# Attention's queries and keys split into high and low parts behind their projections, stored so, with memory of its own for every second pair of heads

## The chip, the core and the metric

The kernel runs on one core of a Trainium2 chip. Four of its engines compute: PE (matrix products, with PEld, the loading of the stationary operand, beside it), DVE (vector work), ACT (activation functions and scaled copies) and POOL. SP mostly issues transfers. Each engine works through its own instructions in the order in which they stand, and waits where an operand, or the memory that it writes, isn't free; what stands behind a waiting instruction waits too. The metric is the device time of one execution in microseconds (us), the median of several runs.

## What is computed

One decoder layer on 1024 tokens of width 1024, in float32. After a normalisation one projection gives the columns of two groups of heads: eight attention heads (queries, keys and values, 64 wide each) and eight heads of a recurrent mixer (RWKV-7). Both results are joined, projected (`w_out`), added to the input, and a feed-forward block follows.

```python
h = _rms_norm(x, norm_mix_pre[i])
z = h @ w_in_first
q = z[..., 0:D_ATTN]; k = z[..., D_ATTN:2 * D_ATTN]; v = z[..., 2 * D_ATTN:3 * D_ATTN]
...
attn = _rms_norm(_dilated_attention(q, k, v), attn_out_gain[i])   # causal, masked scores / sqrt(64)
rw = _rwkv7(r_r, k_r, v_r, ...)
x = x + _rms_norm(jnp.concatenate([attn, rw], axis=-1) @ w_out[i], norm_mix_post[i])
f = jnp.square(jax.nn.relu(_rms_norm(x, norm_ffn_pre[i]) @ w_ffn_up[i])) @ w_ffn_down[i]
x = x + _rms_norm(f, norm_ffn_post[i])
```

## The kernel before, in words

**Split operands.** A float32 product is made from parts in the faster type fp32r: a high part (a copy that rounds) and a low part (the difference). For the big products three matmuls add up high x high, low x high and high x low (`mm3`). Attention's scores need two: for each head the tile `qs` holds in its partitions 0 to 63 the high part of the scaled query and in 64 to 127 its low part, and `kh` and `kl` hold the key's high and low part in both halves, so that one matmul against `kh` and one against `kl` give all four products.

**Stages.** The program runs through the projections with the recurrent mixer woven in, attention, the output projection with the two normalisations (`pm`, `mxa`, `mxr`, `h2t`), and the feed-forward block up (`X`, `Y`, `Z`) and down (`dX`, `dY`, `dZ`).

**Projections.** Each slab of 128 columns is projected in two halves of 512 tokens, 24 matmuls each, into a PSUM bank of the tag `z` (two banks). `proj_spill` empties the bank: for attention's slabs (`aq`, `ak`, `av`, four of each, numbers 12 to 23) ACT copies the half into an SBUF tile of the tag `ev` (three buffers, shared with the mixer's values), and an ACT-queue transfer stores it in DRAM (`zs_d`). A planner (`drive`) that counts estimated times writes down in which order PE takes the mixer's pieces and the projections. PE's order is as written, there and in attention; the order on the other engines, SP among them, is made by a scheduler from the dependencies and priorities.

**Attention.** The eight heads are four pairs p = 0 to 3. A pair has 16 steps m: eight blocks i of 128 queries times two heads h. For a step `at_s` makes the scores (two matmuls into `pS` for each 512 keys; DVE adds the mask `stripT` and keeps the minimum in one instruction; ACT takes the exponential of the row S and its sum), `at_t` turns the row by PE transposes into `pT`, in banks `a` and `c`, one each, which ACT (bank `a`) and DVE (bank `c`, from the fourth block on) copy to `PT`. After every second block `at_v` multiplies by the values into `po`. Scores are made two steps ahead of the transposes, within a pair; at a pair's end, the next pair's first two scores stand behind the last transposes. The values of a pair are loaded as `vT` and turned (`vt`, `Vt`) by `at_vt`.

**Loading a pair** (`at_load`). For each head two transfers bring the query from `zs_d` into both halves of a tile `qr`. POOL writes the scaled high part to `qs` (line 855), DVE overwrites its lower half by the difference (line 856). Two transfers bring the key into `kr`, POOL writes `kh` (line 132), DVE writes `kl` (line 865). The tiles `raw`, `qs`, `kh`, `kl` have two buffers for each tag, one for each head, so that a tile of the next pair can be written only when the last scores of the present pair have read it. `at_load(p + 1)` stands at step 1 of pair p.

**Woven in.** Between attention's steps PE takes the rest of the last projection (steps 0 to 7), and in pairs 2 and 3 parts of the output projection that need only the mixer (`r_ahead`, matmuls `pm`). The weights of the output projection (`WO`) are loaded and split at fixed steps by `load_wo`; four of them, and the tiles of the mix, lie where the projection's input `hT` was (`open_mix`).

Of the kernel before, what the change touches and what calls it, by code (L numbers as in the profile page):

```python
# [8 lines left out]
F32 = mybir.dt.float32  # L9
# [31 lines left out]
def hybrid_kernel(tc, x, par, cst, strip, win, wup_lora, gup, gnwb, grow, wout, wup, wdown, out, dbg=None):  # L41
# [22 lines left out]
    with (  # L64
# [52 lines left out]
        bk_d = dp.tile([8, P, 2, 4, P], F32, name="bk_d")  # L117
        v_d = dp.tile([S, 512], F32, name="v_d")
# [228 lines left out]
        def gate():  # L347
            for t in range(8):
                pg = ps.tile([P, 512], F32, name=f"g{t}", tag="w")
                tt = slice(t * P, (t + 1) * P)  # L350
                mm3(pg, sgh[:, tt], sgl[:, tt], gh, gl, True, True)
                go = evp.tile([P, 512], F32, name=f"go{t}", tag="ev", bufs=3)
                A.activation(go, pg, AF.Copy)
                nc.scalar.dma_start(g_d[t * P:(t + 1) * P, :], go)
                yield 0.7, 0.7
# [318 lines left out]
        def v_out(p, hf):  # L674
# [8 lines left out]
            vt = evp.tile([P, 512], F32, name=f"vt{p}_{hf}", tag="ev", bufs=3)  # L683
            vc = evp.tile([P, 512], F32, name=f"vc{p}_{hf}", tag="ev", bufs=3)
# [8 lines left out]
        def proj_spill(nm, i, shift):  # L693
            last = [None]

            def ev(hf, pz):
                zt_ = evp.tile([P, 512], F32, name=f"ev_{nm}_{hf}", tag="ev" if i >= 8 else "kr", bufs=3 if i >= 8 else 8)
# [147 lines left out]
        at, sx, pts, pos = {}, {}, {}, {}  # L845

        def at_load(p):

            QS, KH, KL = [], [], []
            for h in range(2):  # L850
                qr = ap_.tile([P, S], F32, name=f"qr{p}_{h}", tag="raw")
                for d in range(2):
                    nc.sync.dma_start(qr[own[d]], zs_d[12 + p, h * 64:h * 64 + 64, :])
                qs = ap_.tile([P, S], F32R, name=f"qs{p}_{h}", tag="qs")
                G.tensor_scalar(qs, qr, -0.125, 0.0, op0=OP.mult, op1=OP.add)
                V.scalar_tensor_tensor(qs[64:128], qr[64:128], -0.125, qs[64:128].bitcast(F32), OP.mult, OP.subtract)
                QS.append(qs)
            for h in range(2):
                kr = ap_.tile([P, S], F32, name=f"kr{p}_{h}", tag="raw")
                for d in range(2):  # L860
                    nc.sync.dma_start(kr[own[d]], zs_d[16 + p, h * 64:h * 64 + 64, :])
                kh = ap_.tile([P, S], F32R, name=f"kh{p}_{h}", tag="kh")
                kl = ap_.tile([P, S], F32R, name=f"kl{p}_{h}", tag="kl")
                gcopy(kh, kr)
                V.tensor_tensor(kl, kr, kh.bitcast(F32), OP.subtract)
                KH.append(kh)
                KL.append(kl)
            at[p] = QS, KH, KL

        def at_vt(p):  # L870
            vT = ap_.tile([P, S], F32, name=f"vT{p}", tag="raw")
# [8 lines left out]
        def at_s(p, i, h):  # L880
# [9 lines left out]
            for k in range(nbk):  # L890
                lo, hi = 512 * k, min(w, 512 * k + 512)
                pS = ps.tile([P, 512], F32, name=f"pS{p}_{i}_{h}_{k}", tag="wz"[k] if p == 1 or p == 2 and i < 6 else "w")
# [62 lines left out]
        def open_mix():  # L955
            ev_ctx.__exit__(None, None, None)
            left.__exit__(None, None, None)
            M["tc"] = tc.tile_pool(name="tcomb", bufs=1)
            M["tp"] = M["tc"].__enter__()
            M["mc"] = tc.tile_pool(name="mix", bufs=2)  # L960
            M["mp"] = M["mc"].__enter__()
# [31 lines left out]
        def mix_x1(t, pm, y=None):  # L993
# [5 lines left out]
            if y is None:  # L999
                y = mp.tile([P, D], F32, name=f"y{t}", tag="y")  # L1000
# [58 lines left out]
        def r_ahead(i, keep):  # L1059
# [14 lines left out]
            part[i] = M["mp"].tile([P, D], F32, name=f"y{ORD[i]}", tag="y")  # L1074
# [4 lines left out]
        LEAD = 28  # L1079
        for _ in range(LEAD):  # L1080
            next(rest, None)
        hi_pri = lambda: tc.high_priority(offset=PRI[3])
        step = lambda m: (m // 16, m % 16 // 2, m % 2)
        with hi_pri():
            at_load(0)
            at_s(*step(0))
            at_s(*step(1))
            at_vt(0)
        for m in range(64):
            p, i, h = step(m)  # L1090
            with hi_pri():
                if i == 7:
                    at_t(p, i, h)
                    if h == 0:
                        at_v(p, 4)
                    else:
                        if p < 3:
                            at_s(p + 1, 0, 0)
                            at_s(p + 1, 0, 1)
                            at_v(p, 6)  # L1100
                            at_vt(p + 1)
                else:
                    at_s(p, (m % 16 + 2) // 2, h)
                    at_t(p, i, h)
                    if h == 1 and i in (2, 4):
                        at_v(p, i - 2)
                    if h == 1 and i == 0 and p < 3:
                        at_load(p + 1)
# [5 lines left out]
            if m in (13, 21) or m in (29, 37):  # L1114
                k = {13: 4, 21: 5, 29: 6, 37: 7}[m]
                load_wo(k, w2p, "w2")
            if m == 31:
                open_mix()
            if m in (43, 45, 47, 49):
                load_wo((m - 43) // 2, M["tp"], "woA")  # L1120
            for i_, m0 in ((0, 45), (1, 53)):
# [11 lines left out]
        tp, tp_ctx, mp, mix_ctx = M["tp"], M["tc"], M["mp"], M["mc"]  # L1133
# [120 lines left out]
        mix_ctx.__exit__(None, None, None)  # L1254
        if "x1" in dbg:
# [261 lines left out]
```

## Time and profile before

| | |
|---|---|
| median of three runs | 1368.56 us (1368.4 to 1368.89) |
| the profiled execution | 1369.49 us, its span from the first to the last instruction 1367.7 us |
| busy in the span | PE 1291.0 us (94%), DVE 914.4 us, ACT 626.3 us, POOL 45.9 us |
| PE busy, 200 to 500 us (projections) | 287.4 of 300 us |
| PE busy, 500 to 600 us (attention) | 78.4 of 100 us |
| PE busy, 800 to 1300 us (feed-forward) | 499.6 of 500 us |
| granted PE clock, 500 to 600 us | 0.93; 1.00 from 650 to 1300 us |

The profile gives one execution. A row of the timeline shows when a group of equal instructions started, how long it ran from its first start to its last end, and in brackets how long the engine stood idle before it and what ended that wait. Matmuls overlap, so a row's duration reaches a little into the next row. The chain of waits follows the program back from its last instruction to what released each step; in it a stretch of matmuls has just the time that it adds.

### The profile page before, as it was taken

The page shows a single profiled execution, that of the slowest core. Times are in us where ns is not written, and L with a number is a line of the kernel's source. Part 1 is how long each engine was busy: PE and PEld are TensorE (multiplying, and loading weights), DVE is VectorE, ACT ScalarE, POOL GpSimd, SP SyncE. Part 2 cuts the span into 40 slices and gives each one's busy share as a digit, 9 for nine tenths or more (in the row PEclk, how much of TensorE's full clock was granted, in tenths as well). Part 3 has the DMA queues.
Part 4 walks back from the last instruction along what each step waited for, and adds up shares of the span by engine and source line. Part 5 has one row for each costly group of instructions (what it writes and reads, how often), then busy time and mean ns, then how long its engine had stood idle before and what let it go on. Part 6 is the DMA issues. An engine that isn't in the chain of part 4 may idle for free.

```text
span 1367.7 us, 23518 instructions
## 1 busy us (share of the span) xinstructions
PE 1291.0 (94%) x9360; PEld 1063.5 (78%) x9360; DVE 914.4 (67%) x1647; ACT 626.3 (46%) x1026; POOL 45.9 (3%) x56
## 2 busy tenths in 40 slices
PE   6999999999999988789998999999999999999997
PEld 5777888788777867678787788888888888888875
DVE  7867757531678576555698986777666776445686
ACT  7652324233455376455556444444343444443442
POOL 0000000000000101010000000000000002000110
PEclk9999999999999999999999999999999999999999
DMA  6346747676584663321333344443456995346554
GB/s 253 114 169 162 193 107 195 184 203 211 169 248 147 200 211 91 86 70 40 123 123 133 137 169 170 153 145 135 161 200 211 327 349 182 92 128 210 187 204 165
DMA packets 161197, 231.09 MB, mean 169 GB/s; under 512 B 51680, under 2 KB 88800, under 8 KB 161088
## 3 DMA queue, kind: packets, MB, share of 16 engines
q1 hardware_dynamic: 153024, 208.62, 47.2%
q10 hardware_dynamic: 8064, 20.98, 4.5%
q8 instruction: 73, 1.20, 0.4%
q14 instruction: 36, 0.29, 0.1%
HBM read 156.66 MB, written 72.89 MB: 168 GB/s over the span
## 4 chain that ended last, share of the span: by engine, by line
PE 74%; DVE 13%; DMA 6%; ACT 4%; issue 2%; SPq 0%; POOL 0%; DVEq 0%; ACTq 0%; POOLq 0%
PE X L47 11%; PE dX L47 8%; PE Z L47 6%; PE pm L47 6%; PE dZ L47 5%; PE z_aq L47 3%; PE dY L47 3%; PE z_av L47 3%; PE po L47 3%; PE z_ak L47 3%; PE Y L47 3%; PE z_v L47 3%; PE z_k L47 3%; PE pT L908 2%; PE pS L47 2%
## 5 line engine op out<-in xcount | busy, mean ns | idle before, releaser
L47 PE MATMUL dX<-wow,wou 128*128 128x512 f32 x768 | 176.2, 390 | 2.3 <-DVE wow L1179 1.6
L47 PEld LDWEIGHTS dX<-wow,wou 128*128 128x128 f32 x768 | 143.8, 188 | 34.1 <-DVE wow L1179 3.4
L47 PE MATMUL dZ<-wow,wou 128*128 128x512 f32 x384 | 87.4, 389 | 0.0
L47 PEld LDWEIGHTS dZ<-wow,wou 128*128 128x128 f32 x384 | 72.1, 188 | 15.0
L1178 ACT ACTIVATE wow<-wd 128x1024 fp32r<-128x1024 f32 x40 | 42.3, 1060 | 88.9 <-PE dZ L47 29.8
L1179 DVE TENSOR_TENSOR wou<-ur,wou 128x1024 fp32r<-128x1024 f32 x56 | 72.0, 1287 | 8.4 <-ACT wou L1178 8.3
L1179 DVE TENSOR_TENSOR wow<-wd,wow 128x1024 fp32r<-128x1024 f32 x40 | 49.9, 1250 | 34.7 <-ACT wow L1178 34.1
L1178 ACT ACTIVATE wou<-ur 128x1024 fp32r<-128x1024 f32 x56 | 58.5, 1048 | 20.9 <-DMA ur<-u_d 13.4
L908 PE MATMUL pT<-cst,S 128*128 128x128 f32 x288 | 47.1, 290 | 18.4 <-DVE PT L912 12.2
L898 ACT ACTIVATE S<-S,mn 128x128 f32<-128x128 f32 (+7 forms) x64 | 49.4, 772 | 19.2 <-DVE mn L896 18.4
L908 PEld LDWEIGHTS pT<-cst,S 128*128 128x128 f32 x288 | 34.4, 146 | 28.7 <-issue 11.1
L1265 ACT ACTIVATE r<-u 128x512 f32<-128x512 f32 x48 | 30.0, 626 | 52.4 <-DVE u L1263 52.0
L896 DVE CUSTOM_DVE_ANT_0 S<-pS,stripT 128x512 f32<-128x512 f32 (+3 forms) x64 | 37.6, 590 | 23.5 <-PE pS L47 18.6
L47 PE MATMUL pm<-WO,mxr 128*128 128x512 f32 x192 | 49.4, 400 | 0.5 <-DVE mxr L972 0.5
L47 PE MATMUL z_aq<-hT,wh_aq 128*128 128x512 f32 x128 | 46.5, 417 | 3.5 <-DVE ev_v L202 3.5
L1179 DVE TENSOR_TENSOR wow<-TK,wow 128x1024 fp32r<-128x1024 f32 x16 | 20.8, 1301 | 38.9 <-ACT wow L1178 38.9
L47 PE MATMUL z_k<-hT,wh_k 128*128 128x512 f32 x128 | 44.9, 412 | 1.7 <-DVE z L233 1.4
L47 PE MATMUL Z<-HB,wo 128*128 128x512 f32 x192 | 46.1, 389 | 0.0
L47 PE MATMUL pm<-WO,mxa 128*128 128x512 f32 x192 | 45.8, 394 | 0.0
L47 PE MATMUL X<-HB,wo 128*128 128x512 f32 x180 | 43.6, 390 | 1.6 <-ACT HB L1034 1.6
L47 PE MATMUL z_av<-hT,wh_av 128*128 128x512 f32 x128 | 44.9, 405 | 0.0
L910 ACT ACTIVATE PT<-pT 128x512 f32<-128x512 f32 (+3 forms) x64 | 32.8, 512 | 26.0 <-PE pT L908 17.2
(388 smaller groups left out, 3097.0 us busy)
## 6 DMA issues: line engine op xcount, KB each, us to landing
ur<-u_d SPq DMA_DIRECT2D x56, 512.0 KB, 4.3
wd<-in_wdown_dram SPq DMA_DIRECT2D x40, 512.0 KB, 4.2
u_d<-S SPq DMA_DIRECT2D x64, 256.0 KB, 2.1
u_d<-u SPq DMA_DIRECT2D x48, 256.0 KB, 2.1
wr_upa<-in_wup_dram SPq DMA_DIRECT2D x16, 512.0 KB, 3.6
wr_upb<-in_wup_dram SPq DMA_DIRECT2D x16, 512.0 KB, 4.0
TK<-in_wdown_dram SPq DMA_DIRECT2D x16, 512.0 KB, 7.3
x<-in_x_dram SPq DMA_DIRECT2D x8, 512.0 KB, 8.1
```

Of the source, the lines that this page charges most:

```text
L47: return PE.matmul(o, lhsT, rhs, start=start, stop=stop, skip_group_check=True)
L896: V.tensor_tensor_reduce(Sx[:, lo:hi], pS[:, :hi - lo], stripT[:, so:so + hi - lo], 1.0, 3e38 if k == 0 else mn[:, 0:1], OP.add, OP.min, a ...
L898: A.activation(Sx[:, :w], Sx[:, :w], AF.Exp, scale=-1.0, bias=mn[:, nbk - 1:nbk], accum_out=at[p, "den"][:, i, h:h + 1])
L908: PE.transpose(pt[:, j], Sx[:, (4 * k + j) * P:(4 * k + j + 1) * P], ident)
L910: A.activation(PT[:, 0:nb_], pt[:, 0:nb_], AF.Copy)
L1178: A.activation(w[:, 0, 0:n], raw, AF.Copy)
L1179: E.tensor_tensor(w[:, 1, 0:n], raw, w[:, 0, 0:n].bitcast(F32), OP.subtract)
L1265: A.activation(r, src, AF.Relu)
```

## The change

**The split moves.** When a half of a query or key slab comes out of the projection (`12 <= i < 20`), ACT writes its high part to a tile of fp32r (for the query with the factor -0.125), DVE writes the low part from the PSUM bank and the high part, and both are stored in a new DRAM tensor `qk_d`, the high part by ACT's queue and the low part by POOL's queue. The tag `ev` gets four buffers in place of three, and a half of a query or key takes two of them. `at_load` only loads: 12 transfers of 256 KB for a pair (before 8), straight into `qs`, `kh`, `kl`. POOL's and DVE's splits in attention are gone, and so are the tiles `qr` and `kr`.

**Two sets of tiles.** Each tile has one buffer for each head and set; pairs 0 and 2 use the set in attention's pool, pairs 1 and 3 a set in a new pool `attn1`, which lies where `hT` was. Pair 1 is loaded at step 7 of pair 0, pairs 2 and 3 at step 1 of the pair before. The pool `mix` opens only after attention.

**The order of attention's steps.** The scores of step m + 2 now stand ahead of the transposes of step m across the ends of pairs too. The last `at_v` and the values' `at_vt` come at step 1 of the next pair. The scores use banks of the tags `w` and `z` from the fifth block of pair 0 on; before, they did in pair 1 and a part of pair 2. The weights and `r_ahead` have other steps: `r_ahead(0)` starts at step 39 (before 45), `r_ahead(1)` at 48 (before 53).

```diff
+        qk_d = dp.tile([8, 2, P, S], F32, name="qk_d")
...
             def ev(hf, pz):
+                hs_ = slice(hf * 512, hf * 512 + 512)
+                if 12 <= i < 20:
+                    sc = -0.125 if i < 16 else 1.0
+                    zh, zl_ = (evp.tile([P, 512], F32R, name=f"ev{c_}_{nm}_{hf}", tag="ev", bufs=4) for c_ in "hl")
+                    A.activation(zh, pz, AF.Copy, scale=sc)
+                    V.scalar_tensor_tensor(zl_, pz, sc, zh.bitcast(F32), OP.mult, OP.subtract)
+                    A.dma_start(qk_d[i - 12, 0, :, hs_], zh.bitcast(F32))
+                    G.dma_start(qk_d[i - 12, 1, :, hs_], zl_.bitcast(F32))
+                    return
...
         def at_load(p):
-            QS, KH, KL = [], [], []
+            at[p] = QS, KH, KL = [], [], []
             for h in range(2):
-                qr = ap_.tile([P, S], F32, name=f"qr{p}_{h}", tag="raw")
-                for d in range(2):
-                    nc.sync.dma_start(qr[own[d]], zs_d[12 + p, h * 64:h * 64 + 64, :])
-                qs = ap_.tile([P, S], F32R, name=f"qs{p}_{h}", tag="qs")
-                G.tensor_scalar(qs, qr, -0.125, 0.0, op0=OP.mult, op1=OP.add)
-                V.scalar_tensor_tensor(qs[64:128], qr[64:128], -0.125, qs[64:128].bitcast(F32), OP.mult, OP.subtract)
-                QS.append(qs)
-            for h in range(2):
-                kr = ap_.tile([P, S], F32, name=f"kr{p}_{h}", tag="raw")
...
-                gcopy(kh, kr)
-                V.tensor_tensor(kl, kr, kh.bitcast(F32), OP.subtract)
...
+                hs_ = slice(64 * h, 64 * h + 64)
+                for L, nm, q, js in ((QS, "qs", p, (0, 1)), (KH, "kh", 4 + p, (0, 0)), (KL, "kl", 4 + p, (1, 1))):
+                    t = aset[p % 2].tile([P, S], F32R, name=f"{nm}{p}_{h}", tag=f"{nm}{h}", bufs=1)
+                    for d in range(2):
+                        nc.sync.dma_start(t[own[d]].bitcast(F32), qk_d[q, js[d], hs_, :])
+                    L.append(t)
...
-                pS = ps.tile([P, 512], F32, name=f"pS{p}_{i}_{h}_{k}", tag="wz"[k] if p == 1 or p == 2 and i < 6 else "w")
+                pS = ps.tile([P, 512], F32, name=f"pS{p}_{i}_{h}_{k}", tag="wz"[k if i > 3 else h] if p > 0 or i > 4 else "w")
...
+                if m + 2 < 64:
+                    at_s(*step(m + 2))
+                at_t(p, i, h)
+                if h == 1 and i % 2 == 0 and m > 1:
+                    at_v(*((p, i - 2) if i else (p - 1, 6)))
+                if h == 1 and i == 0:
+                    at_vt(p)
+                if m == 17 or m == 33:
+                    at_load(p + 1)
...
-            for i_, m0 in ((0, 45), (1, 53)):
+            for i_, m0 in ((0, 39), (1, 48)):
```

Three places show how the instructions move. In the names the first digit is the pair, then come the block and the head; ISA is DVE's instruction that adds the mask and takes the minimum (its second row reads the minimum out).

DVE at the end of pair 1, before:

```order
L896 ISA S1_7_0_5980,mn1_7_0_5981<-pS1_7_0_1_5986,stripT_5030,mn1_7_0_5981 128x512
L896 ISA mn1_7_0_5981 128x1
L856 SCALAR_TENSOR_TENSOR qs2_0_5732<-qr2_0_5729,qs2_0_5732 64x1024
L896 ISA S1_7_1_6003,mn1_7_1_6004<-pS1_7_1_0_6005,stripT_5030 128x512
L896 ISA mn1_7_1_6004 128x1
L856 SCALAR_TENSOR_TENSOR qs2_1_5738<-qr2_1_5735,qs2_1_5738 64x1024
L896 ISA S1_7_1_6003,mn1_7_1_6004<-pS1_7_1_1_6009,stripT_5030,mn1_7_1_6004 128x512
L896 ISA mn1_7_1_6004 128x1
L912 COPY PT1_6_0_5991<-pT1_6_0_1_5998 128x384
L912 COPY PT1_6_1_6014<-pT1_6_1_1_6021 128x384
```

And now:

```order
L894 ISA S1_7_0_6016,mn1_7_0_6017<-pS1_7_0_1_6022,stripT_5070,mn1_7_0_6017 128x512
L894 ISA mn1_7_0_6017 128x1
L910 COPY PT1_6_0_6027<-pT1_6_0_1_6034 128x384
L894 ISA S1_7_1_6039,mn1_7_1_6040<-pS1_7_1_0_6041,stripT_5070 128x512
L894 ISA mn1_7_1_6040 128x1
L946 SCALAR_TENSOR_TENSOR WO3_6878<-wo3_6876,par_76,WO3_6878 128x1024
L894 ISA S1_7_1_6039,mn1_7_1_6040<-pS1_7_1_1_6045,stripT_5070,mn1_7_1_6040 128x512
L894 ISA mn1_7_1_6040 128x1
L910 COPY PT1_6_1_6050<-pT1_6_1_1_6057 128x384
```

The two splits of the next pair's query, for which DVE waited on POOL, are gone; the copy that empties the bank `c` (PT1_6_0) has moved ahead of the last scores; the split of one output weight (WO3) has come in.

PE at the same place, before:

```order
L47 MATMUL po1_1_6044<-Vt1_5694,PT1_5_1_5969 64x64 x12
L908 MATMUL pT1_7_1_0_6090<-cst_75,S1_7_1_6003 128x128 x4
L908 MATMUL pT1_7_1_1_6096<-cst_75,S1_7_1_6003 128x128 x4
L47 MATMUL pS2_0_0_0_6106<-kh2_0_5744,qs2_0_5732 128x128
L47 MATMUL pS2_0_0_0_6106<-kl2_0_5745,qs2_0_5732 128x128
L47 MATMUL pS2_0_1_0_6113<-kh2_1_5751,qs2_1_5738 128x128
L47 MATMUL pS2_0_1_0_6113<-kl2_1_5752,qs2_1_5738 128x128
L47 MATMUL po1_1_6044<-Vt1_5694,PT1_6_0_5991 64x64 x14
```

And now:

```order
L47 MATMUL po1_1_6062<-Vt1_5755,PT1_5_1_6005 64x64 x12
L47 MATMUL pS2_0_0_0_6111<-kh2_0_5771,qs2_0_5768 128x128
L47 MATMUL pS2_0_0_0_6111<-kl2_0_5774,qs2_0_5768 128x128
L906 MATMUL pT1_7_0_0_6117<-cst_75,S1_7_0_6016 128x128 x4
L906 MATMUL pT1_7_0_1_6123<-cst_75,S1_7_0_6016 128x128 x4
L47 MATMUL pS2_0_1_0_6131<-kh2_1_5780,qs2_1_5777 128x128
L47 MATMUL pS2_0_1_0_6131<-kl2_1_5783,qs2_1_5777 128x128
L906 MATMUL pT1_7_1_0_6137<-cst_75,S1_7_1_6039 128x128 x4
L906 MATMUL pT1_7_1_1_6143<-cst_75,S1_7_1_6039 128x128 x4
L47 MATMUL pS2_1_0_0_6151<-kh2_0_5771,qs2_0_5768 128x256
```

The next pair's scores have moved ahead of the present pair's last transposes, and the last products with the values (po1 with PT1_6 and PT1_7) have moved behind the next pair's first transposes.

SP's queue of transfers at the start of attention, before:

```order
L853 DMA qr0_0_5141<-zs_d_92 64x1024 x2
L853 DMA qr0_1_5147<-zs_d_92 64x1024 x2
L843 DMA stripT_5030<-in_strip_dram 128x1024
L861 DMA kr0_0_5153<-zs_d_92 64x1024 x2
L861 DMA kr0_1_5160<-zs_d_92 64x1024 x2
L943 DMA wo6_6026<-in_wout_dram 128x1024
```

And now:

```order
L865 DMA qs0_0_5190<-qk_d_95 64x1024 x2
L865 DMA kh0_0_5193<-qk_d_95 64x1024 x2
L865 DMA kl0_0_5196<-qk_d_95 64x1024 x2
L865 DMA qs0_1_5199<-qk_d_95 64x1024 x2
L865 DMA kh0_1_5202<-qk_d_95 64x1024 x2
L870 DMA vT0_5249<-zs_d_92 128x1024
L865 DMA kl0_1_5205<-qk_d_95 64x1024 x2
L853 DMA stripT_5070<-in_strip_dram 128x1024
L941 DMA wo6_6271<-in_wout_dram 128x1024
```

The mask `stripT` was the fifth transfer and is now the fourteenth, behind all 12 loads of pair 0 and its values.

65 lines of the change are left out of this document (23 added, 42 removed).

## The prediction

> **What bounds the kernel now.** I read the stage windows first, then PE's timeline where it stands idle, then the other engines at those moments, and the chain of waits last. Over most of the program PE simply has work. Attention is the exception. Windows for pairs 0 to 3 of it (bounds, length, busy time of each engine with its instructions, granted PE clock, share and rate of the transfers):
>
> ```profile
> 479.00:522.00 43.00, 36.90 (x437) 30.48 (x437) 30.10 (x73) 28.57 (x61) 5.27 (x4) 0.92 0.67 213
> 522.00:564.50 42.50, 32.72 (x424) 27.57 (x420) 24.98 (x66) 22.86 (x52) 4.68 (x4) 0.92 0.27 76
> 564.50:606.00 41.50, 33.45 (x429) 27.27 (x425) 25.71 (x67) 23.23 (x53) 4.30 (x4) 0.96 0.25 71
> 606.00:646.00 40.00, 39.14 (x471) 33.91 (x468) 21.02 (x61) 26.15 (x54) 0.00 (x0) 1.00 0.11 35
> ```
>
> The columns are PE, PEld, DVE, ACT, POOL. Pairs 1 and 2 keep PE idle for 9.8 and 8.1 us, at a clock below 1. Pair 3, which loads no successor and has `pm` matmuls woven in, has 0.9 us and the full clock. No engine is full in pairs 0 to 2, so the time goes into waiting. PE's longest waits there, all at the ends of pairs 0, 1 and 2:
>
> ```profile
> 510.41 2.68 PE L908 MATMUL pT<-cst,S 128*128 128x128 f32 x11 [3.60 <-DVE PT L912]
> 550.34 2.64 PE L908 MATMUL pT<-cst,S 128*128 128x128 f32 x11 [3.85 <-DVE PT L912]
> 559.13 0.33 PE L47 MATMUL pS<-kl,qs 128*128 128x128 f32 x1 [1.84 <-DVE kl L865]
> 590.97 0.52 PE L908 MATMUL pT<-cst,S 128*128 128x128 f32 x3 [1.26 <-DVE PT L912]
> 593.39 0.66 PE L908 MATMUL pT<-cst,S 128*128 128x128 f32 x4 [1.02 <-DVE PT L912]
> 599.29 0.33 PE L47 MATMUL pS<-kh,qs 128*128 128x128 f32 x1 [0.60 <-POOL kh L132]
> 600.55 0.33 PE L47 MATMUL pS<-kl,qs 128*128 128x128 f32 x1 [0.93 <-DVE kl L865]
> ```
>
> These sum to 13.1 us. Why the copy of `PT` is late shows on POOL and DVE at the end of pair 1:
>
> ```profile
> 544.43 1.05 POOL L855 TENSOR_SCALAR qs<-qr 128x1024 fp32r<-128x1024 f32 x1 [28.89 <-PE pS L47]
> 546.13 1.54 POOL L855 TENSOR_SCALAR qs<-qr 128x1024 fp32r<-128x1024 f32 x1 [0.65 <-PE pS L47]
> 545.55 1.22 DVE L856 SCALAR_TENSOR_TENSOR qs<-qr,qs 64x1024 fp32r<-64x1024 f32 x1
> 547.71 1.22 DVE L856 SCALAR_TENSOR_TENSOR qs<-qr,qs 64x1024 fp32r<-64x1024 f32 x1 [0.21 <-POOL qs L855]
> 549.64 0.55 DVE L912 COPY PT<-pT 128x384 f32<-128x384 f32 x1
> ```
>
> POOL had waited 28.89 us for a buffer that pair 1's last scores still read. Once it is free, POOL's copy, DVE's two splits and the scores between them stand ahead of the copy from bank `c` (549.64), and PE's next transposes need that bank. What costs time is not the work of the splits but their place, which the shared buffers force to the end of the pair.
>
> **The slow stretch behind a wait.** PE also runs slower for some us after these waits. The chain of waits, at the ends of pairs 0, 1, 2 and, undisturbed, 3 (start, us, what):
>
> ```profile
> 510.41 2.68 PE pT L908 x11
> 513.09 4.07 PE po L47 x88
> 517.16 1.02 PE pT L908 x8
> 550.34 2.64 PE pT L908 x11
> 552.98 3.01 PE po L47 x88
> 555.99 1.04 PE pT L908 x8
> 559.46 5.20 PE po L47 x120
> 600.88 5.20 PE po L47 x120
> 637.88 2.71 PE po L47 x88
> 641.18 0.87 PE pT L908 x8
> 642.05 3.65 PE po L47 x120
> ```
>
> The measure is pair 3: 0.87 for eight transposes (so 1.20 for eleven), 2.71 for x88, 3.65 for x120. End of pair 0: 1.48 + 1.36 + 0.15 = 2.99 us too long. Pair 1: 1.44 + 0.30 + 0.17 + 1.55 = 3.46. Pair 2: 1.55. Together 8.0 us, which no row calls idle.
>
> [...]
>
> **The change part by part.**
>
> *Splits out of attention.* Their reason to stand at the pairs' ends is gone: pairs 1 and 3 have tiles of their own, pair 2 is loaded 12 to 13 steps early, and DVE has no part in it. I take back both sums, 13.1 + 8.0 = 21.1 us, less a rest: the split of one output weight, WO3, now stands among pair 1's last scores. A row of this kind on DVE:
>
> ```profile
> 510.18 1.27 DVE L948 SCALAR_TENSOR_TENSOR WO<-wo,par,WO 128x1024 fp32r<-128x1024 f32 x1
> ```
>
> The rest lies between 0 (the copy is on time) and 3.8 (as much as 1.27 at each of three ends); I take 1.1, near the low end, because `PT1_6_0` moved ahead of the last scores and only one end has such a split. **-20.0 us.**
>
> *Steps ahead across pairs.* The first steps of a pair, and its blocks 5 and 6, have waits of their own:
>
> ```profile
> 524.51 0.33 PE L908 MATMUL pT<-cst,S 128*128 128x128 f32 x1 [1.01 <-ACT Vt L878]
> 528.47 0.55 PE L908 MATMUL pT<-cst,S 128*128 128x128 f32 x3 [0.75 <-ACT PT L910]
> 543.00 0.41 PE L908 MATMUL pT<-cst,S 128*128 128x128 f32 x2 [1.51 <-DVE PT L912]
> ```
>
> They come from single banks (`a`, `c`) that ACT and DVE empty, and these stay single. So **0**; the bound on the good side is all three in pairs 1 and 2, at most 2 x 3.3 = 6.6. The wider use of `z` banks for scores lies beside this and costs nothing.
>
> *`r_ahead` earlier.* The same `pm` matmuls fill pair 2's second half in place of pair 3's. Pair 3 then has bare steps at its end, like pair 1, whose blocks 5 and 6 lost 1.51; pair 2 gains the like. **0**, between -1.5 and 1.5.
>
> *Loading pair 0.* Rows that carry it (SP's queue, DVE, the ACT-queue stores, and the last projections on the chain):
>
> ```profile
> 460.75 2.38 SPq L853 DMA_DIRECT2D qr<-zs_d  x4
> 467.69 3.61 SPq L861 DMA_DIRECT2D kr<-zs_d  x4
> 479.40 0.29 DVE L896 CUSTOM_DVE_ANT_0 S<-pS,stripT 128x128 f32<-128x128 f32 x1 [0.58 <-PE pS L47]
> L709 ACTq DMA_DIRECT2D zs_d<-ev_aq x8: 326/330/398, 255.7 to 463.2; - x8
> DMA to landing us min/median/max: 2.4/4.1/6.5
> 450.63 10.88 PE z_aq L47 x48
> ```
>
> The first load waits for the stores of pair 3's first query half, whose `ev` memory it takes over. That half leaves PE at 456.1 (450.63 + 10.88 / 2). ACT's copy and store of it let the first load go 4.7 us later, at 460.75. The low part comes 0.7 us behind (DVE's subtraction, 0.68, below) and lands after 2.4 to 6.5 us if POOL's queue is like ACT's, whose median is 4.1: the first load goes out between 460 and 464, I take 462. Then 14 transfers to `stripT` at 0.6 to 0.9 us each (2.38 and 3.61 for four): 470.4 to 474.6; with 4.1 to 6.5 us to land, the mask is there at 474.5 to 481. DVE needs it at 479.40. **+1.0**, between 0 and 4. SP's other work behind this (weights, pair 1) is not due before 490, when the last projection frees `hT`. Pair 1's 12 loads then take 7 to 11 us to issue and 4 to 6.5 to land, 501.5 to 507.5; its first scores stand before 510.41 less the 3.60 saved, plus 2.7 of `po`: about 509. Hidden, by a hair.
>
> *Splits in the projections.* ACT's copies and stores stay. DVE gets 16 subtractions from PSUM, like the first row, in a stage where PE is 96% busy:
>
> ```profile
> L972 DVE TENSOR_TENSOR mxr<-mxtr,mxr x8: 640/682/692, 593.5 to 718.9; 128x512 fp32r<-128x512 f32 x8
> PE O L47 <- DVE HV L641: 3.3, 3, 1.7
> 300.00:400.00 100.00, 96.84 (x1331) 78.50 (x1327) 51.94 (x117) 43.94 (x74) 0.00 (x0) 1.00 0.67 204
> ```
>
> 16 x 0.68 = 10.9 us of DVE, which is half idle there. PE waits for DVE only in the recurrence (HV, 3.3 us in all, between 200 and 476 us); a subtraction in front of an HV step delays it by up to 0.68. Between 0 and 10.9 (all of them) I take **+1.0**, near the low end by DVE's idle half. The bank `z` is released 0.7 us later, against 5.4 us until the half after next wants it. The extra transfers (4 MB stored, 4 MB loaded) use a share of 0.67 here and 0.27 in pair 1: nothing.
>
> *The mix's pool opens later:* its first tiles (`gpM`, `ma`) wait for pair 3's last scores at about 636, five us or more before their use. 0.
>
> **Sum.** 1369.5 (the profiled execution) - 20.0 + 1.0 + 1.0 = 1351.5. That execution lies 0.9 above the median of the runs, so **1350.5 us**; this case's own range is 1346 to 1356.
>
> **Rivals.**
>
> *More comes back.* The lead of two steps also hides the first steps' waits and those at blocks 5 and 6: up to 6.6 more, 1344. For it: the exponentials now start ahead of the pair. Against: the releasers named are the copies out of single banks.
>
> *The waits form anew.* ACT is busy for 23 us of a pair; in one of 33.3 us (42.5 less 3.85, 1.84 and 3.46) it works at 69%, in order, and PE waits for its copies. If half of the waits and of the slow stretches return, 10.5 us are lost: 1361. For it: 0.75 <-ACT PT in the rows. Against: pair 3 has ACT 26.15 of 40 us and no wait.
>
> *Loads land late.* Pair 1's data miss 509 by up to 5 us, and a slow stretch of 3 follows: 1358.5.
>
> *Slower: the stores on POOL's queue hold up the projections.* A half takes two of the four `ev` buffers, so its buffers must be free two halves later, 10.9 us (450.63, x48 is two halves). After 1.3 us of ACT and DVE a store has 9.6 us. Above that each of 16 halves waits: from about 10.8 us to land, 16 x 1.2 = 19 us eat the gain; at 12 us the time is 1350.5 + 16 x 2.4 = 1389. For it: no row shows a POOL store. Against: 6.5 us is the longest on ACT's queue.
>
> [...]
>
> **How the numbers follow.** Forecast 0.54, more 0.14, waits anew 0.14, late loads 0.10, slower 0.08. About 0.2% (2.7 us) is what a measurement of this kernel tells from no change. Of the slower rival's weight 0.06 lies beyond that bound and 0.02 within; 0.01 of the others too: faster 0.91, same 0.03, slower 0.06. The range 1343 to 1362 leaves out the slower rival and the tails.
>
> **What would show it.** Right: pair 1 in 32 to 35 us from its `vt` to the next, no wait over 1.5 us for `PT` at their ends, granted clock 0.98 or more, x120 at 3.65; the stage before 479 within 2 us. Wrong: waits for `qs`, `kl` or the mask at a pair's first scores; `z` or `O` waiting for `ev` tiles between 250 and 480; POOL stores that take over 9 us.

## The result, and the profile after

The changed kernel takes **1351.75 us** (median of four runs, 1348.41 to 1356.3), where the kernel before took 1368.72 beside it: a ratio of 0.9877, with a 95% interval of 0.984 to 0.991. Forecast were 1350.5 us and a range of 1343 to 1362. Time and direction came out as forecast; of the steps behind them one had its cause only half right and one was mis-sized, and their errors nearly cancel.

The four pairs in the profiled execution (1348.41 us; windows from the first scores to the last output; columns as in the prediction: length, PE, PEld, DVE, ACT, POOL, granted clock, share and rate of the transfers):

```profile
477.10:520.00 42.90, 36.54 (x441) 30.23 (x441) 25.67 (x73) 29.77 (x67) 0.00 (x0) 0.96 0.79 224
520.00:553.20 33.20, 29.54 (x424) 24.69 (x420) 20.81 (x63) 23.49 (x53) 0.00 (x0) 1.00 0.76 199
553.20:590.90 37.70, 35.55 (x456) 30.06 (x452) 21.46 (x64) 24.73 (x56) 0.00 (x0) 1.00 0.26 78
590.90:625.60 34.70, 32.98 (x447) 28.84 (x442) 19.49 (x55) 22.37 (x45) 0.00 (x0) 1.00 0.19 63
```

Pairs 1 to 3 are 9.3, 3.8 and 5.3 us shorter, at the full clock; pair 0 is as long as it was. Attention took 166.7 us (479.0 to 645.7) and takes 148.5. PE's waits in it, before:

```profile
PE pT L908 <- DVE PT L912: 12.2, 7, 3.9
PE pT L908 <- ACT Vt L878: 2.9, 4, 1.0
PE pS L47 <- DVE kl L865: 2.8, 2, 1.8
```

and after (us in all, times, longest; both from 470 to 660 us):

```profile
PE pT L906 <- DVE PT L910: 4.2, 4, 1.5
PE pS L47 <- DVE mn L894: 2.4, 3, 1.4
PE pT L906 <- ACT Vt L876: 2.0, 3, 0.9
PE pS L47 <- DMA kl<-qk_d: 1.5, 1, 1.5
```

The wait for DVE's copy of `PT` is 8.0 us shorter, the splits' `kl` is gone, and one wait is new: `kl` from the transfers. All rows of the view added up, PE waited 25.3 us before and 14.2 after. The end of pair 0 on PE's timeline:

```profile
509.08 0.52 PE L906 MATMUL pT<-cst,S 128*128 128x128 f32 x3 [0.74 <-DVE PT L910]
509.53 2.79 PE L47 MATMUL po<-Vt,PT 128*64 128x64 f32 x88
...
514.14 1.09 PE L906 MATMUL pT<-cst,S 128*128 128x128 f32 x8 [0.39 <-ACT PT L908]
...
516.59 3.72 PE L47 MATMUL po<-Vt,PT 128*64 128x64 f32 x120
```

Before, 3.60 us of waiting stood ahead of the x88, and it took 4.07 (4.14 as this timeline counts); now the wait is 0.74 and the x88 takes 2.79. The new cost stands at the start of attention (PE, then SP's queue):

```profile
479.00 0.30 PE L47 MATMUL pS<-kl,qs 128*128 128x128 f32 x1 [1.50 <-DMA kl<-qk_d]
480.74 0.39 PE L47 MATMUL pS<-kh,qs 128*128 128x256 f32 x1 [1.45 <-DVE mn L894]
```

```profile
459.47 1.10 SPq L865 DMA_DIRECT2D qs<-qk_d  x2
...
473.30 1.08 SPq L865 DMA_DIRECT2D kl<-qk_d  x2
474.43 0.59 SPq L853 DMA_DIRECT2D stripT<-in_strip_dram  x1
```

The last loads of `kl` go out only at 473.30 and the mask behind them; PE waits 1.50 us for the one and 1.45 for the minimum, which needs the other.

### The profile page after: what moved, and what is told of

Read it like the earlier page. It is cut to its first block, busy times and chain, and to the rows that moved or that the text cites. A ratio compares the mean times of both kernels' runs of the same rounds, so it can differ in the third digit from the quotient of the medians.

```text
span 1346.3 us, 23565 instructions
## 1 busy us (share of the span) xinstructions
PE 1280.9 (95%) x9360; PEld 1056.4 (78%) x9360; DVE 903.5 (67%) x1647; ACT 624.8 (46%) x1026; POOL 36.2 (3%) x56
## 4 chain that ended last, share of the span: by engine, by line
PE 72%; DVE 12%; DMA 8%; ACT 4%; issue 3%; SPq 1%; DVEq 0%; ACTq 0%
PE X L47 12%; PE dX L47 9%; PE Z L47 6%; PE pm L47 6%; PE dZ L47 5%; PE dY L47 3%; PE z_v L47 3%; PE z_aq L47 3%; PE Y L47 3%; PE z_k L47 3%; DMA bv<-v_d 2%; PE po L47 2%; PE pT L906 2%; PE z_av L47 2%; PE z_r L47 2%
## 5 line engine op out<-in xcount | busy, mean ns | idle before, releaser
L47 PE MATMUL z_v<-hT,wh_v 128*128 128x512 f32 x128 | 42.9, 400 | 1.0 <-DVE ev_r L203 1.0
```

The lines of the kernel that those rows point to most:

```text
L47: return PE.matmul(o, lhsT, rhs, start=start, stop=stop, skip_group_check=True)
```

## Taking a run apart: stages and the clock

Single runs of one kernel differed by up to 17 us here, more than most of the questions. The traces say why. In the traces of the kernel before and of the changed one each stretch at a clock of 0.50 begins a whole number of pieces of 3.41 us behind the first (16 to 378 of them before, 33 to 356 in the changed kernel) and lasts one or two pieces, except the last, which runs to the end; and each follows a piece at full clock in which PE was busy for at most 1.88 us. Windows cut on that grid, the kernel before at the ends of pairs 0 (the first line) and 1:

```profile
509.21:512.63 3.42, 2.22 (x10) 2.01 (x11) 3.42 (x7) 1.24 (x2) 1.04 (x1) 0.50 0.89 224
...
546.76:550.17 3.41, 0.00 (x0) 0.00 (x0) 3.14 (x7) 0.93 (x3) 0.92 (x1) 1.00 0.52 156
550.17:553.59 3.42, 3.25 (x23) 2.75 (x25) 0.69 (x3) 0.89 (x2) 1.04 (x1) 0.50 0.59 153
...
557.00:560.41 3.41, 1.57 (x39) 1.36 (x39) 2.33 (x6) 1.19 (x5) 0.00 (x0) 1.00 0.43 155
560.41:563.83 3.42, 3.42 (x72) 3.42 (x68) 0.00 (x0) 0.00 (x0) 0.00 (x0) 0.50 0.55 150
```

PE stood for all of the piece from 546.76, and for 1.84 of the one from 557.00 (busy 1.57): behind both the clock is 0.50 for just one piece, which loses half of 3.41, 1.7 us. So a wait of 1.84 us within one piece was enough there, and the grid lies elsewhere against the program from one execution to another: a piece begins 1.01 us behind the first scores in the changed kernel (478.07) and 2.45 us behind them in its second execution (487.54). The bound is not sharp: 1.88 us of work lost the clock (597.96, before), 1.70 kept it (751.56, before), and so did 1.57 (730.66, changed kernel), which had lost it above. Behind a piece that itself ran at half clock, 2.22 us of work (509.21, above) were followed by a second such piece, 3.04 (481.49, changed kernel) by full clock. Some pieces do not follow this at all: at the start of the program two in which PE did nothing (0.63 and 4.04, before) were followed by full clock; why is open.

So each profiled execution is taken apart below by the trace's records: the projections (from the first `z_aq` to the first scores) and attention (to the last output), each less the half of its pieces at half clock; and that loss, in attention and in the rest of the program. (us)

| kernel | projections | attention | clock loss in attention | clock loss elsewhere | span |
|---|---|---|---|---|---|
| before | 233.1 | 158.1 | 8.5 | 11.1 | 1367.7 |
| changed | 234.6 | 146.8 | 1.7 | 7.5 | 1346.3 |
| changed, again | 234.4 | 146.1 | 3.4 | 16.3 | 1356.4 |
| low halves stored by ACT | 234.8 | 148.8 | 1.7 | 16.4 | 1356.0 |
| mask first | 234.3 | 145.7 | 3.4 | 10.7 | 1348.9 |
| no low parts made | 232.9 | 146.7 | 1.7 | 10.0 | 1347.4 |
| pair 3's high halves by POOL | 235.7 | 146.3 | 1.7 | 18.4 | 1355.5 |
| late splits, own memory | 232.4 | 150.9 | 5.1 | 12.4 | 1355.7 |
| early splits, shared memory | 234.9 | 159.3 | 20.5 | 12.6 | 1382.0 |
| no lead, pair 2 early | 234.4 | 158.8 | 6.8 | 9.8 | 1366.1 |
| no lead | 236.1 | 157.3 | 1.7 | 12.7 | 1361.2 |
| no lead, output later | 234.6 | 150.6 | 3.4 | 13.1 | 1354.7 |
| pair 0 in column halves | 234.6 | 144.1 | 1.7 | 13.4 | 1346.9 |
| filler at the start | 233.7 | 148.7 | 0.0 | 11.6 | 1347.7 |

The stretches ahead of these two and behind them stay within 3.1 us over all rows, the half of slow pieces taken off. Nine rows share the changed kernel's code of the projections: seven lie between 234.3 and 234.9, the others at 233.7 and 236.1, so one execution gives this length to some 1.5 us, far better than the whole time.

## The experiments

**The changed kernel again**

> The changed kernel once more, unchanged. Its four executions so far took 1348.41, 1349.14, 1354.36 and 1356.3 us, where the kernel before spread by 1.6. If the spread belongs to the change (theory S1: it brings a wait that some executions have and others not), two groups near 1349 and 1355 come again, and before stays within 2 us. If it was the hour on that chip (S2), all executions now lie within 2 us of each other.

1355.47 us (median of six, 1353.1 to 1358.73), ratio 0.989 (0.985 to 0.993). Before, on the same chip, spread from 1364.59 to 1381.3 in eleven runs, so the spread is not the change's. Neither S1 nor S2 as written: what differs between the two traces is how much the clock lost. This execution has the first one's lengths within 0.7 us in both stages, yet lost 10.5 us more to the clock; its span is 10.1 longer. The clock at its first scores:

```profile
484.12:487.54 3.42, 1.41 (x8) 1.07 (x7) 0.00 (x0) 0.40 (x1) 0.00 (x0) 1.00 0.91 174
487.54:490.95 3.41, 1.68 (x6) 1.40 (x7) 0.92 (x6) 1.07 (x5) 0.00 (x0) 0.50 0.99 392
490.95:494.36 3.41, 3.05 (x13) 2.45 (x12) 1.60 (x5) 2.93 (x9) 0.00 (x0) 0.50 0.79 316
```

Two pieces in a row are less than half busy (1.41 and 1.68), so two are slow; in the first execution it was one.

**The low halves stored by ACT's queue**

```diff
-                    G.dma_start(qk_d[i - 12, 1, :, hs_], zl_.bitcast(F32))
+                    A.dma_start(qk_d[i - 12, 1, :, hs_], zl_.bitcast(F32))
```

> The low halves are stored by ACT's queue in place of POOL's. If POOL's queue makes the spread (S1a) or holds the projections' buffers, all executions lie near 1348.5 and spread by less than 2 us. If POOL's queue costs nothing (the theory: POOL's stores landed after 5.1 to 5.5 us where ACT's took 4.5 to 5.3), the median stays within 2 us of the changed kernel's and the spread stays as it is; ACT pays 16 issues more.

1354.67 us, ratio 0.9885 (0.985 to 0.992): POOL's queue makes neither the spread nor a cost in the projections (234.8). Attention is 2 to 3 us longer because the first scores wait 3.8 us for `kl`.

**The mask ahead of pair 0's loads**

```diff
-        nc.sync.dma_start(stripT, strip)
...
+            nc.sync.dma_start(stripT, strip)
             at_load(0)
```

> The mask's transfer is issued ahead of pair 0's loads in place of behind them. In the changed kernel PE waited 1.50 us for kl and 1.45 us for the first block's minimum (which needed the mask, issued at 474.43 us, landed 5.8 us later), and ran at a clock of 0.92 for 20 us behind. If the mask is late (theory M), the 1.45 goes and with it some 1 to 2 us of slow clock: 2 to 3 us faster. If kl, whose last loads go out at 473.30, is as late (rival K), the wait only changes its name: within 1 us. If the spread comes from this place (S1b), it shrinks below 3 us.

1352.74 us, ratio 0.987 (0.983 to 0.991). The waits only change hands, as rival K has it: 1.14 us for `kh` and 1.44 for `kl` in place of 1.50 and 1.45. Attention at full clock is 145.7, at most 1.1 us shorter.

**Without the low parts in the projections**

```diff
-                    V.scalar_tensor_tensor(zl_, pz, sc, zh.bitcast(F32), OP.mult, OP.subtract)
...
-                    G.dma_start(qk_d[i - 12, 1, :, hs_], zl_.bitcast(F32))
```

> The projections no longer make and store the low parts: 16 subtractions on DVE and 16 stores on POOL's queue are left out, and the loads of attention fetch the high part twice, so that as much is moved. This changes the scores. The forecast's term for the splits in the projections is +1.0 us: 0.5 to 1.5 us faster than the changed kernel. If the term was far too small (up to 10.9), 5 us or more faster. If DVE's or POOL's share of it makes the spread (S1a), the executions lie within 2 us of each other.

1348.7 us, ratio 0.985 (0.981 to 0.990). The whole time cannot say 1 from 3 us. The stage says 232.9 in place of 234.6 and 234.4, 1.6 us, hardly more than one row's spread; but the three kernels here that make no low parts in the projections have 232.4 to 233.1, and the eleven that do 233.7 to 236.1. PE's waits in the projections, changed kernel and then this one:

```profile
PE O L47 <- DVE HV L642: 3.3, 2, 2.1
...
PE O L47 <- DMA T<-ar_d: 1.9, 2, 1.3
```

```profile
PE O L47 <- DVE HV L642: 2.3, 3, 1.2
PE O L47 <- DMA T<-ar_d: 1.0, 2, 0.8
```

1.0 us less through DVE, 0.9 less through transfers that the mixer waits for; beside the kernel before, only the second kind had grown (`HV` 3.3 there too, `T` 0.6). The spread stays (1345.84 to 1357.0).

**Pair 3's high halves by POOL's queue**

```diff
-                    A.dma_start(qk_d[i - 12, 0, :, hs_], zh.bitcast(F32))
+                    (G if i % 4 == 3 else A).dma_start(qk_d[i - 12, 0, :, hs_], zh.bitcast(F32))
```

> The high halves of pair 3's queries and keys are stored by POOL's queue too. In the changed kernel the last loads of pair 0 share a completion counter with ACT's store of evh_ak3_0 and wait for it, from 467.9 to 473.3 us, although they need nothing of it; behind them stands the mask. Theory C: without that store on the counter the loads go out by 470, and both waits at the first scores (1.5 to 3.8 for kl, 0.9 to 1.5 for the minimum) go, and with them the one or two windows of half clock behind (1.7 us each): 4 to 6 us faster than the changed kernel. Rival D: the data land late anyway, or another transfer holds them: within 1.5 us.

1355.34 us, ratio 0.989 (0.987 to 0.991). The loads no longer stop for ACT's store, yet the waits stay, at 0.84 us for `kl` and 1.52 for the minimum: rival D. Why shows in the transfers while pair 0 is loaded, here:

```profile
474.00:479.00 5.00, 5.00 (x24) 4.14 (x23) 1.00 (x2) 0.60 (x1) 1.08 (x2) 1.00 1.04 315
479.00:484.00 5.00, 5.00 (x24) 4.14 (x23) 0.69 (x1) 0.60 (x1) 1.08 (x2) 1.00 1.02 346
```

The transfers' share is 1.04 and 1.02 (and 1.03 in the next 5 us). The last two `kl` are issued from 7.2 us behind the first load on, in place of 13.8, but `kl` takes longer to land (median 7.8 us, 5.4 in the changed kernel).

**Pair 0 in halves of columns**

```diff
+                for c in range(2):
+                    cs = slice(512 * c, 512 * c + 512)
...
+                                nc.sync.dma_start(L[h][own[d], cs].bitcast(F32), qk_d[q, js[d], hs_, cs])
+                        if h == 0:
+                            ss = slice(512 - 512 * c, 1024 - 512 * c)
+                            nc.sync.dma_start(stripT[:, ss], strip[:, ss])
```

> Pair 0's tiles and the mask are loaded in two halves of 512 columns, the half that the first four blocks need ahead of the other. While pair 0 is loaded the DMA engines' share is 0.98 to 1.05 for 15 us (before: 0.90 to 0.96), so theory B has it that the amount is what is late (12 x 256 KB and 2 x 512 KB at 290 to 380 GB/s): with half as much ahead, the waits for kl (1.5 to 3.8) and the minimum (0.9 to 1.5) at the first scores go, and the window or two of half clock behind them (1.7 us each): span times granted clock 2 to 3 us below the changed kernel's 1336.4, the time 3 to 6 us below. If the counters or SP's 14 more issues hold the loads (rival D), the waits stay and it is within 1.5 us.

**1349.11 us** (1345.31 to 1351.8), ratio 0.985 (0.982 to 0.987). Theory B holds: from 470 to 500 us no row for `kl` is left, and

```profile
PE pT L920 <- ACT PT L922: 1.1, 1, 1.1
PE pS L47 <- DVE mn L908: 0.3, 2, 0.2
```

are all of PE's waits there, 1.4 us where the changed kernel had 4.3. No piece at half clock follows the first scores. Attention is 144.1 us, 2.0 to 2.7 less than the changed kernel's, its clock loss 1.7 (behind a wait at 504 us). By its ratio to the kernel before this is the fastest version here; on whole times the intervals of its ratio and the changed kernel's still overlap, so it is the stage that carries the verdict.

**Filler at the first scores**

```diff
+                if p == 0 and i == 0 and h == 1:
+                    for _ in range(12):
+                        mm(pS, hT[:, 0, 0, 0:P], hT[:, 0, 0, 0:512], True, True)
```

> Twelve matmuls of 128x512 that compute nothing (their bank is overwritten) stand on PE ahead of the second head's first scores, 2.6 us of work where PE waits 3 us for kl and the mask. In the traces so far the granted clock changes on a fixed grid of 3.41 us, and a piece of that grid in which matmuls run for less than about half of it is followed by one at half clock. Theory H (it is this, not the length of any one wait): the half-clock piece at the start of attention is gone, the clock between the first scores and 15 us behind is 1.00 (0.93 in the changed kernel), the x3 of z_av there take 0.22 us each, not 0.4, and 1.5 to 3.4 us are gained although work was added. If the clock follows waits as such, or the matmuls delay the loads' consumers, no gain or 1 us more.

1351.99 us, ratio 0.988 (0.985 to 0.991). The same stretch on the grid, changed kernel:

```profile
478.07:481.49 3.42, 1.02 (x5) 0.70 (x6) 0.72 (x5) 0.77 (x4) 0.00 (x0) 1.00 1.00 382
481.49:484.90 3.41, 3.04 (x12) 2.36 (x12) 1.68 (x5) 2.81 (x10) 0.00 (x0) 0.50 0.90 359
```

with the filler:

```profile
477.89:481.30 3.41, 2.23 (x12) 1.66 (x11) 0.89 (x6) 0.90 (x5) 0.00 (x0) 1.00 1.02 413
481.30:484.71 3.41, 2.44 (x17) 2.02 (x16) 1.72 (x5) 3.41 (x9) 0.00 (x0) 1.00 0.72 288
```

Theory H holds for the clock: busy for 2.23 of 3.41, and the clock stays; attention loses nothing to it. The 1.5 to 3.4 us that it was to gain did not come. The filler itself lengthened attention at full clock by 1.9 to 2.6 us, so that it is as long as the changed kernel's in all (148.7 and 148.5): the useless work paid for itself by the clock and no more.

**Late splits into own memory**

```diff
-                if 12 <= i < 20:
+                if i < 0:
...
+                qs = aset[p % 2].tile([P, S], F32R, name=f"qs{p}_{h}", tag=f"qs{h}", bufs=1)
+                G.tensor_scalar(qs, qr, -0.125, 0.0, op0=OP.mult, op1=OP.add)
+                V.scalar_tensor_tensor(qs[64:128], qr[64:128], -0.125, qs[64:128].bitcast(F32), OP.mult, OP.subtract)
```

> Own memory without the early splits: the projections store the plain queries and keys as the kernel before did, and attention splits them as it did (POOL copies, DVE subtracts, 1.2 us each), but into the tiles that every second pair has for itself, 12 to 13 steps ahead. Theory P (it is the place that counts, and memory frees the place): the waits for PT at the pairs' ends stay away as in the changed kernel, and span times granted clock, which was 1336.4 us for the changed kernel and 1348.2 for the one before (medians), is 1333 to 1338, since DVE's 5 us per pair lie beside other work and the projections lose nothing. Rival W (it is the work taken from DVE and POOL): the copies of PT stay late behind DVE's splits, and it is 1342 to 1348.

1357.57 us, ratio 0.9895 (0.987 to 0.992). Theory P in the main: without any early split most of the gain stays (7.2 us of attention's 11.3 at full clock). The splits in attention are not free, though:

```profile
PE pT L917 <- DVE PT L921: 7.1, 6, 2.0
PE pS L47 <- DVE mn L905: 3.9, 4, 2.0
PE vt L886 <- ACT PT L919: 2.4, 1, 2.4
```

Attention is 4.1 to 4.8 us longer than the changed kernel's, the projections 2.0 to 2.2 shorter: moving the split ahead is worth some 2 to 3 us at full clock.

**Early splits, one set of tiles**

```diff
-            aset[1] = M["ac"].__enter__()
+            M["ac"].__enter__(); aset[1] = ap_
...
-                if m == 17 or m == 33:
+                if m in (13, 29, 45):
```

> Early splits without own memory: all pairs use the same six tiles, and a pair's twelve loads follow the last scores of the pair before. Theory P: only two steps of a pair cover 7 to 11 us of issuing and 4 to 6 us of landing, so that PE stands for 8 to 12 us at each of three ends and runs at half clock for one or two windows behind each: 30 to 45 us slower than the changed kernel, slower than before. Rival W (the work that was taken out is what counts): no more than 10 us slower than the changed kernel, and still faster than before.

1383.69 us, ratio 1.009 (1.007 to 1.011): 28 us slower than the changed kernel by the ratios and slower than before. The order of steps is the changed kernel's. PE waits for loads at each pair's end,

```profile
PE pS L47 <- DMA kl<-qk_d: 12.1, 7, 2.4
PE pS L47 <- DMA kh<-qk_d: 8.9, 4, 3.6
```

21.0 us (18.6 without the 2.40 of pair 0's start), and the clock loses 20.5 us in attention. The stops are shorter than theory P had them, the slow clock behind them worse, and the whole is a little less than its 30 to 45.

**The old order at the pairs' ends**

```diff
-                if m + 2 < 64:
+                if m % 16 < 14:
                     at_s(*step(m + 2))
                 at_t(p, i, h)
...
+                if m % 16 == 14:
+                    at_v(p, 4)
+                if m % 16 == 15 and p < 3:
+                    at_s(p + 1, 0, 0)
+                    at_s(p + 1, 0, 1)
+                    at_v(p, 6)
+                    at_vt(p + 1)
```

> The order of steps at the pairs' ends as the kernel before had it (no lead of two steps across pairs, transposes of V behind the last output), all else as changed. The forecast priced the lead at 0: span times granted clock within 1.5 us of the changed kernel's 1336.4, with new waits of less than 1 us at the pairs' starts. The rival that more comes back has its gain from the lead: then 3 to 6.6 us slower here. If the lead in truth brings much of the gain (theory L: scores of the next pair cover the copy of the last PT), the PT waits of 2 to 4 us return and it is 6 to 12 us slower.

1371.26 us, ratio 1.001 (0.999 to 1.003): none of the gain is left. But a wait of 6.93 us for `kl` stands at pair 1's first scores, because pair 2's loads had come free early and stood among pair 1's in SP's queue. So once more, with those loads later:

```diff
-                if m == 17 or m == 33:
+                if m == 25 or m == 41:
```

> The old order of steps at the pairs' ends again, now with pair 2 and 3 loaded at step 25 and 41 (in the run before, pair 2's loads had come free early and stood among pair 1's, which were then 6.93 us late). The late loads and two windows of half clock were worth some 7 + 3 us of that run's 13 to 15. If the lead as such is worth nothing (the forecast's term of 0), this one is within 2 us of the changed kernel: span times granted clock 1335 to 1338. If the lead hides ACT's copies at the pairs' starts (waits for ACT PT were 5.1 us in 9 there, 0.6 in 2 in the changed kernel's pair 0), it stays 3 to 6 us above, 1339 to 1343. If it carries the gain (theory L), 1346 or more.

1366.0 us, ratio 0.997 (0.995 to 0.999). Attention at full clock is 157.3 us, 10.5 more than the changed kernel's and 0.8 less than before. DVE's `PT` has 4.9 us (4.2 in the changed kernel), and no wait for a split is left, but others took their place:

```profile
PE po L47 <- issue: 5.5, 2, 3.0
PE pT L906 <- DVE PT L910: 4.9, 5, 1.5
PE pT L906 <- ACT PT L908: 3.9, 7, 0.8
```

The first are two stops in the middle of x120,

```profile
519.18 3.37 PE L47 MATMUL po<-Vt,PT 128*64 128x64 f32 x108
525.13 0.57 PE L47 MATMUL po<-Vt,PT 128*64 128x64 f32 x12 [2.58 <-issue]
...
562.31 1.62 PE L47 MATMUL po<-Vt,PT 128*64 128x64 f32 x48 [2.95 <-issue]
...
598.40 3.72 PE L47 MATMUL po<-Vt,PT 128*64 128x64 f32 x120
```

where the engine waits for nothing that the profile shows. The order alone does not bring them: pair 2's x120 stands in the same order here and runs through (the last line), and so did pair 0's in the kernel before (3.72 from 518.51). One thing was then put back, the place of x120:

```diff
                     at_s(p + 1, 0, 1)
-                    at_v(p, 6)
-                    at_vt(p + 1)
+                if m % 16 == 1 and p > 0:
+                    at_v(p - 1, 6)
+                    at_vt(p)
```

> The order of the run before this one (no scores ahead of a pair's last transposes, pair 2 and 3 loaded at steps 25 and 41) with one thing taken from the changed kernel: a pair's last output (x120) and the transposes of V stand behind the first two transposes of the next pair, not right behind the pair's own last transposes. Between the first scores and the last output, with the half-clock loss taken off, PE took 158.1 us in the kernel before, 146.8 in the changed one and 157.3 without the lead; 5.5 of the last lay in two stops in the middle of x120, which no wait explains. Theory O (the place of x120 is what the lead brings: the copies of the last PT and the fetch of its instructions get time): 147 to 150 here, no stops, and a time within 2 us of the changed kernel's. Theory S (the scores ahead are what counts, the stops were an accident of that kernel): 151 to 154.

1359.72 us, ratio 0.993 (0.991 to 0.995); attention 150.6, between the two theories' bands, and the time not within 2 us of the changed kernel's. The stops are gone and x120 runs through:

```profile
517.69 3.72 PE L47 MATMUL po<-Vt,PT 128*64 128x64 f32 x120
```

Of the 10.5 us, 6.7 came back with the place of x120 (the stops' 5.5 among them), and 3.8 are what is left: the scores ahead of the last transposes, and with them x88 one step earlier and the earlier loads of pairs 2 and 3. Both theories had a part. Each of these lengths is from one execution.

## Why the prediction was right, and where not

**What bounds the kernel, and the waits at the pairs' ends: right.** None of the seven waits quoted there is left above 0.74 us, PE's waits in attention fell by 11.1 us and attention at full clock by 11.3 to 12.0, with 12.0 forecast (13.1 less a rest of 1.1). Pair 1 took 33.2 us from its `vt` to the next (32 to 35 forecast), and x120 takes 3.72 at the ends of pairs 1 and 2 in place of 5.26 and 5.27 (all by the timeline, whose rows are a little longer than the chain's; at the end of pair 0 it had taken 3.72 before, too).

**"Splits out of attention": the number right, its cause only half.** The step credited the whole 20.0 us to splits that leave the pairs' ends, and gave the **steps ahead across pairs** 0. The runs share it out otherwise. Early splits and the lead without own memory lose time (1383.69). Early splits and own memory with the old order at the ends bring 0.8 us at full clock, and 6.8 of the clock's loss (1.7 in place of 8.5). The 5.5 us of stops count against that kernel; since the kernel before has the same x120 without them, the 0.8 may be low for memory and the 10.5 high for the lead. The rival "the waits form anew" has that size (10.5), but not the way: waits for ACT's copies are 3.9 us in place of 1.4, the stops are more, and half clock did not return. The lead brings 3.8 by the scores ahead and 6.7 by the later x120, and 5.5 of these are the stops. With memory and lead, moving the splits early adds some 2 to 3. So memory lets the lead stand, and of the 18.1 us by which attention got shorter (slow clock included) 10.5 came only with the lead on top; the lead with the splits and the memory of the kernel before was not run. The rows for the lead (1.01 `Vt`, 1.51 `PT`) were read rightly, since these waits are still there; what they could not show is the waits that would come once the splits were out of the way. That the sum held is luck in this step: the lead, priced at 0, was in the same change.

**The slow stretch behind a wait: right in kind.** 8.0 us were read off x88, x8 and x120; five pieces at half clock are 8.5. All five are gone. But one or two new ones stand at the first scores (1.7 and 3.4 us): "granted clock 0.98 or more" held for pairs 1 to 3 (1.00), while pair 0 had 0.96. And in the rest of the program the loss was 7.5 and 16.3 in two executions of the same kernel. That a measurement tells 0.2% was too hopeful for the same reason: the intervals here reach 0.4% to either side.

**"Loading pair 0", +1.0: mis-sized.** PE waits 4.3 us from 470 to 500, where it waited 1.7, and 1.7 to 3.4 of slow clock follow: 4.3 to 6.0, above the step's range of 0 to 4. The first load went out at 459.47 (462 was taken); what failed is that "the extra transfers use a share of 0.67 here: nothing". While pair 0 is loaded the share is 1.0 for 15 us. With half of the data ahead the waits were gone. Waits for `kl` and the mask at a pair's first scores were among the prediction's signs of being wrong; they came at pair 0 alone.

**Splits in the projections, +1.0:** 1.3 to 1.5 by the stages, 1.6 by leaving the low parts out. The size was right, the way only in part: the growth beside before is in waits for transfers, which the step held to be nothing. No new wait of `z` for `ev` came (the one of 3.5 us for `ev_v` stands before, too).

**POOL's queue, the slower rival: not so.** Its stores, and ACT's of the same slabs:

```profile
L705 POOL DMA_DIRECT2D qk_d<-evl_aq x8: 539/540/710, 253.1 to 462.7; - x8
DMA to landing us min/median/max: 2.5/5.1/6.2
```

```profile
L704 ACTq DMA_DIRECT2D qk_d<-evh_aq x8: 326/326/352, 248.7 to 461.0; - x8
DMA to landing us min/median/max: 2.0/4.5/5.3
```

The keys' low halves landed after 7.3 at most, all well under the 9.6 from which the rival decides. POOL's medians lie 0.6 us above ACT's for the queries (5.1 and 4.5) and 0.2 for the keys (5.5 and 5.3).

**Pair 1's loads**, "hidden by a hair", were in time: its first scores follow x88 without a wait. `r_ahead`'s new steps were not tried alone; pair 2, which now holds more of its matmuls, took 37.7 us and pair 3 34.7, and a wait of 1.51 for `PT` like pair 1's now stands in pair 3, as the prediction thought it might. The mix's later pool shows no cost: `mxta` waits 1.4 us as before.

The errors nearly cancel, and this is luck: the pairs' ends gave back more than 20.0 (by these terms 11.3 + 2.6 of start waits + 8.5, some 22), the start took 4.3 to 6.0 in place of 1.0, the projections 0.4 more.

## What to carry to other kernels

When a wait is taken away by memory, look up in the new order what stands behind it, for the order may carry the gain; undo order and memory apart before crediting either. Where a stage starts by loading all that it needs, send first the part that its first blocks read. Compare stages at full clock when single runs differ by more than the question.

## What the runs showed of the hardware

In these traces the clock went by pieces of 3.41 us and by how much of a piece PE was busy: 1.41 us (changed kernel, again) did not keep it, 2.23 (filler) did, and between 1.57 and 1.88 us both were seen; to end a stretch at half clock 2.22 was too little (before) and 3.04 enough (changed kernel). Two executions of the same kernel differed by 10.1 us in their spans and by 10.5 in what the clock lost, and useless matmuls in a gap kept the clock at 1.00, where it had been 0.50.

In the second run of the old order x120 stopped twice, for 2.58 and 2.95 us, where the trace names no wait. One transfer of 0.02 MB on the queue that the profile calls `instruction` falls into 522.0 to 523.8 us and one into 559.0 to 561.0, where PE went on at 525.13 and 562.31, and the other transfers' share was 1.00 and 0.97 there; the run before it has a third stop (2.24 us, to 564.18). The first:

```profile
520.00:525.00 5.00, 2.55 (x88) 2.46 (x85) 0.00 (x0) 0.76 (x4) 0.00 (x0) 1.00 1.03 246
```

Where x120 ran through in the same order, the share was 0.62 (517 to 523 us, before), with one such transfer in it, too (518 to 522.3 us). In the changed kernel x88 ran through at shares of 1.05 (509.53 to 512.32 us) and 1.02 (542.69 to 545.48 us). Whether PE had run out of instructions was not tried by itself. The cause stays open.
